# A list of background steps that is empty earns no steps

## The chip, the cores and the metric

One core of a Trainium2 chip runs the whole layer as one program. The metric is device time in microseconds, the median of several executions. The core has five engines that run side by side, each through its own instructions in order: TensorE (PE) for matmuls, VectorE (DVE), ScalarE (ACT), GpSimd (POOL) and SyncE (SP), which here only issues transfers. TensorE's clock is granted in two levels, 1.2 and 2.4 GHz; the profile gives the granted share of full speed.

## The reference

A decoder layer on 512 tokens of width 2048. With h the modulated RMS norm of x, one projection gives q, k, v (8 heads of 128), a forget logit, u (512 wide) and two gates:

```python
q, k, v, f_logit, u, gate_s, gate_a = jnp.split(h @ w_in, IN_SPLIT_POINTS, axis=-1)
y_ssm = half_glu(s5_mixer(u, ...))           # a scan over time, 1024 complex states
y_attn = fox_attention(q, k, v, f_logit, ...)  # head-wise RMS of q and k, causal softmax with a
                                               # bias from the cumulated log forget gate
merged = sigmoid(gate_s) * (y_ssm @ w_ssm_up) + sigmoid(gate_a) * (y_attn @ w_attn_up)
x = x + g1 * (merged @ w_out)
x = x + g2 * peer_ffn(h2, ...)               # product-key experts; most of the time, not touched here
```

## The kernel before, in words

A float32 matmul of the large projections is three matmuls (`mm3`, L88 to L90, and L201 to L203 for the token form): each operand is a rounded high part and the rest, and high x high, high x low and low x high are summed in PSUM.

The part around the change is written in an order by hand (`manual_schedule`): each engine gets its instructions in the order in which the program issues them. It begins after u is projected (about 160 us) and ends with the first pair of gates (about 773 us). Its trunk is the list of projections: the forget logits (`mproj(1)`), then for each of four pairs of heads q, k and v (`mproj_tok`, 256 columns, one result per 128 tokens), then two gates (`mproj(2)`). A projection runs in four units of weights; a unit's parts are quarters. A quarter of `mproj_tok` is 12 matmuls of 256 columns, one of `mproj(2)` 6 of 512. `unit` (L167) issues a part, behind the first part also the high part of the next unit's weights on ScalarE (L158) and their low part on VectorE (L164), and calls `tick` after each part. The stage has 8 + 12 x 16 + 32 = 232 ticks.

`tick` (L111) issues steps of background work. There are three lists (L1869 on), each `[generators, rate, credit]`; a step is what a generator does up to its next `yield`:
- `bpo`, rate 1: `forget` (L807, 11 steps) and `qk` (L838, 11 steps), the head-wise norm of q or k: squares on ScalarE (L846), the reciprocal root (L850 to L858) and the product (L861) on VectorE, eight transposes on TensorE (L867), copies on ScalarE.
- `bat`, rate RH, in the gates RL: two `head`s (L882, 14 steps each): scores on TensorE (L901), bias, mask and maximum on VectorE (L903 to L906), exp on ScalarE (L907), reciprocal (L912) and scaling (L913), transposes (L920), their copies (L922), products with v (L929), and a transfer to `yd` (L936).
- `bs5`, rate RT = 2.0 up to the end of the first q, then R5: the S5 scan (L687), 191 steps: tables, then 16 times (j) 10 steps of products, sums and scans on VectorE, four passes of `bu` (L724) and four of `y` (L732, L733) on TensorE.

q's list gets its generator when q's projection has been issued, k's likewise; the heads of a pair get theirs behind v (L1882). Just before, `flush` (L123) issues at once whatever is left in `bpo` and `bat`; at the end `bat` and `bs5` are flushed. Transposes, scores and the S5 transposes share two PSUM buffers (`tp`). Gelu of S5's result (L944) and the GLU belong to the next part, whose order a planner makes; the casts of the heads' outputs, read back from `yd` (L1899), stand at its start.

Of the kernel before, what the change touches and what calls it, by code (L numbers as in the profile page):

```python
# [38 lines left out]
TODO = ('tg', '', 'tgw', '', 'tg', '', 'tg', 'm')  # L39

RT = 2.0
R5 = 0.92
RH = 0.66
RL = 1.0
GB = (3592, 5640)
PE_ROWS = (2, 3, 5, 6, 7, 12)
NA = 3
# [16 lines left out]
class Builder:  # L64
# [46 lines left out]
    def tick(self):  # L111

        for b in self.bg:
            b[2] += b[1]
            while b[2] >= 1 and b[0]:
                b[2] -= 1
                try:
                    next(b[0][0])
                except StopIteration:
                    b[0].pop(0)  # L120
                    b[2] += 1
# [1002 lines left out]
    def routes(self, es, norm, rows, opened, early):  # L1124
# [45 lines left out]
        for h in range(NH):  # L1170
            pd = [self.t(pq, [P, TM], F32, "pd", bufs=3) for n in range(2)]
            pss = self.t(pq, [P, 256], F32, "ps", bufs=1)
            for j in range(4):
# [28 lines left out]
                for n in range(2):  # L1202
                    for k in range(4):
                        dense(n, k)
                    tick()
                for k in range(4):
                    first(k)
                tick()
            if h == 0:
                ep = opened()  # L1210
# [272 lines left out]
    def experts(self, route):  # L1483
# [5 lines left out]
        with ExitStack() as es:  # L1489
# [146 lines left out]
            def deferred(tick):  # L1636
                nonlocal n, nxt
                ga, nxt = scores(n, nxt, lambda c: tick())
                nc.sync.dma_start(self.gd[n], ga)
                n += 1  # L1640
# [190 lines left out]
    def build(self):  # L1831
# [26 lines left out]
        with tc.manual_schedule():  # L1858
# [15 lines left out]
            for hp in range(4):  # L1874
                qs, ks = [], []
                bpo[0].append(self.qk(self.raw(self.mproj_tok()), self.col2[:, 0:1], qs))
                bs5[1] = R5
                bpo[0].append(self.qk(self.raw(self.mproj_tok()), self.col2[:, 1:2], ks))
# [3 lines left out]
                bat[0].extend(self.head(hp * 2 + i, qs, ks, v) for i in range(2))  # L1882
            bat[1] = RL
            sg = self.gates(0, self.apool, "a")
# [93 lines left out]
```

## Time and profile before

| | us |
|---|---|
| median of 3 runs | 3901.11 (3896.51 to 3903.49) |
| the profiled execution, its own time | 3898.42 |
| its span, first to last instruction | 3896.6 |
| TensorE busy in the span | 3685.5 (95%) |
| VectorE busy | 3030.8 (78%) |
| ScalarE busy | 1305.8 (34%) |
| the stage of the change, 160.0 to 773.2 | 613.2 |
| TensorE busy in it, mean granted clock | 519.2, 0.88 |

Times in the trace are counted from the span's first instruction. A busy share of TensorE counts a matmul from its start to its modelled end, and at half clock a matmul takes twice as long, so the granted clock is read beside it. A wait is idle time of an engine directly before an instruction, put down to what released it last.

### The profile page before, as it was taken

The page shows a single profiled execution, that of the slowest core. Times are in us where ns is not written, and L with a number is a line of the kernel's source. Part 1 is how long each engine was busy: PE and PEld are TensorE (multiplying, and loading weights), DVE is VectorE, ACT ScalarE, POOL GpSimd, SP SyncE. Part 2 cuts the span into 40 slices and gives each one's busy share as a digit, 9 for nine tenths or more (in the row PEclk, how much of TensorE's full clock was granted, in tenths as well). Part 3 has the DMA queues.
Part 4 walks back from the last instruction along what each step waited for, and adds up shares of the span by engine and source line. Part 5 has one row for each costly group of instructions (what it writes and reads, how often), then busy time and mean ns, then how long its engine had stood idle before and what let it go on. Part 6 is the DMA issues. An engine that isn't in the chain of part 4 may idle for free.

```text
span 3896.6 us, 58629 instructions
## 1 busy us (share of the span) xinstructions
PE 3685.5 (95%) x22966; PEld 3375.0 (87%) x22966; DVE 3030.8 (78%) x4731; ACT 1305.8 (34%) x2265; POOL 725.8 (19%) x518
## 2 busy tenths in 40 slices
PE   6888888999999998899989999999999999999998
PEld 2677777777778778889989999999999999999997
DVE  6676665365657438986879999999999988999997
ACT  3323333422223224235644333333333333333332
POOL 0000000000000004423421222222222221222221
PEclk8998888899999999999999999999999999999999
DMA  8511112266777552227889999999999988999996
GB/s 300 178 55 49 49 49 71 76 211 213 219 219 230 157 139 89 69 94 261 299 299 309 327 363 372 367 362 366 372 368 371 369 308 298 369 372 356 371 367 216
DMA packets 467082, 967.39 MB, mean 248 GB/s; under 512 B 66379, under 2 KB 335861, under 8 KB 400117
## 3 DMA queue, kind: packets, MB, share of 16 engines
q1 hardware_dynamic: 411508, 560.97, 43.8%
q0 software_dynamic: 55296, 402.68, 26.6%
q8 instruction: 180, 2.95, 0.3%
q14 instruction: 98, 0.79, 0.1%
HBM read 926.51 MB, written 36.96 MB: 247 GB/s over the span
## 4 chain that ended last, share of the span: by engine, by line
PE 73%; DVE 12%; DMA 8%; ACT 3%; issue 2%; POOL 1%; SPq 0%; DVEq 0%; ACTq 0%; POOLq 0%
PE A L90 7%; PE A L88 7%; PE A L89 7%; PE V L90 7%; PE V L89 7%; PE V L88 7%; PE tp L1538 6%; DMA y<-in_w_ada_dram 5%; PE mm L201 2%; PE mm L203 2%; PE mm L202 2%; DVE y L301 2%; PE mm L88 2%; PE mm L90 2%; PE mm L89 2%
## 5 line engine op out<-in xcount | busy, mean ns | idle before, releaser
L88 PE MATMUL A<-hi,uhi 128*128 128x320 f32 x2048 | 658.1, 321 | 0.0
L88 PE MATMUL V<-ghi,vhi 128*128 128x320 f32 x2048 | 651.9, 318 | 3.3 <-ACT vhi L1518 2.7
L90 PE MATMUL V<-ghi,vlo 128*128 128x320 f32 x2048 | 633.9, 310 | 5.2 <-DVE vlo L1521 5.2
L89 PE MATMUL V<-glo,vhi 128*128 128x320 f32 x2048 | 634.1, 310 | 1.6 <-DVE glo L1599 1.5
L90 PE MATMUL A<-hi,ulo 128*128 128x320 f32 x2048 | 633.4, 309 | 0.0
L89 PE MATMUL A<-lo,uhi 128*128 128x320 f32 x2048 | 633.0, 309 | 0.0
L1542 ACT CAST uhi<-tp 128x512 fp32r<-128x512 f32 x512 | 301.0, 588 | 606.4 <-PE tp L1538 602.7
L1448 DVE SCALAR_TENSOR_TENSOR big<-g,av,big 128x2048 f32<-128x2048 f32 x190 | 445.6, 2345 | 11.7 <-DMA g<-in_peer_v_dram,ids 6.8
L1436 DVE SCALAR_TENSOR_TENSOR g<-g,big 128x2048 f32<-128x2048 f32 x192 | 438.3, 2284 | 16.6 <-DMA big<-hx 6.6
L88 PEld LDWEIGHTS V<-ghi,vhi 128*128 128x128 f32 x2048 | 386.2, 189 | 5.9 <-ACT vhi L1518 3.0
L90 PEld LDWEIGHTS V<-ghi,vlo 128*128 128x128 f32 x2048 | 385.5, 188 | 5.6 <-DVE vlo L1521 5.6
L89 PEld LDWEIGHTS V<-glo,vhi 128*128 128x128 f32 x2048 | 386.4, 189 | 2.7 <-DVE glo L1599 2.6
L89 PEld LDWEIGHTS A<-lo,uhi 128*128 128x128 f32 x2048 | 386.4, 189 | 0.0
L88 PEld LDWEIGHTS A<-hi,uhi 128*128 128x128 f32 x2048 | 386.1, 189 | 0.0
L90 PEld LDWEIGHTS A<-hi,ulo 128*128 128x128 f32 x2048 | 385.1, 188 | 0.0
L1549 DVE TENSOR_TENSOR ulo<-tp,uhi 128x512 fp32r<-128x512 f32 x428 | 291.3, 681 | 58.6 <-ACT uhi L1542 49.8
L94 ACT CAST whi<-wf 128x1024 fp32r<-128x1024 f32 x146 | 153.6, 1052 | 540.3 <-PE mx L89 217.4
L1521 DVE TENSOR_TENSOR vlo<-vf,vhi 128x1024 fp32r<-128x1024 f32 x248 | 302.5, 1220 | 28.2 <-ACT vhi L1518 28.0
L1518 ACT CAST vhi<-vf 128x1024 fp32r<-128x1024 f32 x248 | 259.6, 1047 | 165.4 <-PE V L89 132.5
L1538 PE MATMUL tp<-ident,uf 128*128 128x128 f32 x2048 | 307.7, 273 | 5.0 <-DMA uf<-in_peer_u_dram 4.7
L301 DVE SCALAR_TENSOR_TENSOR y<-y,cond,y 128x512 f32<-128x512 f32 x240 | 192.9, 804 | 148.4 <-DMA y<-in_w_ada_dram 145.3
L1538 PEld LDWEIGHTS tp<-ident,uf 128*128 128x128 f32 x2048 | 255.6, 141 | 15.5 <-issue 5.1
(470 smaller groups left out, 7359.0 us busy)
## 6 DMA issues: line engine op xcount, KB each, us to landing
uf<-in_peer_u_dram SPq DMA_DIRECT2D x128, 1024.0 KB
vf<-in_peer_v_dram SPq DMA_DIRECT2D x248, 512.0 KB
y<-in_w_ada_dram SPq DMA_DIRECT2D x256, 256.0 KB
wf<-in_w_in_dram SPq DMA_DIRECT2D x116, 512.0 KB
wd<-ev SPq DMA_DIRECT2D x40, 512.0 KB
wt<-wd SPq DMA_DIRECT2D x128, 160.0 KB
adaw<-in_w_ada_dram SPq DMA_DIRECT2D x32, 512.0 KB
wf<-in_w_ada_dram SPq DMA_DIRECT2D x32, 512.0 KB
```

The costliest lines, as they stand in the source:

```text
L88: mm(ps, lhi, rhi, start=start, stop=False)
L89: mm(ps, lhi, rlo, start=False, stop=False)
L90: mm(ps, llo, rhi, start=False, stop=stop)
L94: nc.scalar.copy(hi, src)
L301: nc.vector.scalar_tensor_tensor(acc, w, col, acc, op0=ALU.mult, op1=ALU.add)
L1436: V.scalar_tensor_tensor(g, g, 1.0, hr, op0=ALU.mult, op1=ALU.mult, accum_out=av[:, s:s + 1])
L1448: V.scalar_tensor_tensor(acc, g, av[:, s:s + 1], acc, op0=ALU.mult, op1=ALU.add)
L1518: nc.scalar.copy(vhi, vf)
L1521: V.tensor_sub(vlo, vf, vhi.bitcast(F32))
L1538: mm(tp[:, k], ufs[i][:, (4 * c + k) * P:(4 * c + k + 1) * P], self.ident, is_transpose=True, start=k == 0, stop=False, skip_group_check=True)
L1542: nc.scalar.copy(hi, tp)
L1549: late.append(on_pe if i < ND0 - 3 else lambda: V.tensor_sub(lo, tp, hi.bitcast(F32)))
```

## The change

Credit is added only while a list has a generator; while it is empty its credit is 0. Two rates change with it.

```diff
-R5 = 0.92
+R5 = 0.8
 RH = 0.66
-RL = 1.0
+RL = 1.1
...
     def tick(self):
 
         for b in self.bg:
-            b[2] += b[1]
+            b[2] = b[2] + b[1] if b[0] else 0.0
             while b[2] >= 1 and b[0]:
                 b[2] -= 1
                 try:
```

## Rows read from the trace of the kernel before

**Rows 1.** The page: TensorE's granted clock in 40 slices of the span, in tenths.

```profile
PEclk8998888899999999999999999999999999999999
```

**Rows 2.** Busy time by stretch: its length, then each engine (instructions), PEclk, DMA share, GB/s.

```profile
160.00:773.20 613.20, 519.22 (x3083) 435.78 (x3082) 362.30 (x838) 213.94 (x492) 0.00 (x0) 0.88 0.19 59
178.00:229.00 51.00, 34.41 (x195) 27.79 (x194) 44.12 (x97) 14.28 (x40) 0.00 (x0) 0.85 0.14 41
299.20:332.50 33.30, 23.92 (x83) 15.48 (x81) 17.18 (x42) 17.00 (x43) 0.00 (x0) 0.70 0.02 9
...
729.60:773.20 43.60, 43.60 (x189) 35.10 (x188) 15.90 (x19) 16.94 (x24) 0.00 (x0) 1.00 0.38 115
773.20:1240.00 466.80, 459.08 (x2004) 369.65 (x2003) 291.64 (x364) 112.90 (x131) 26.09 (x14) 1.00 0.69 214
```

**Rows 3.** Waits of TensorE, 160 to 773 us: total us, times, longest.

```profile
PE tp L867 <- DVE t L861: 44.9, 8, 7.4
PE tp L901 <- DVE S L903: 13.9, 8, 1.7
PE tp L920 <- ACT PT L922: 11.3, 9, 1.4
...
PE tp L824 <- DVE fz L818: 4.1, 1, 4.1
```

**Rows 4.** Timeline of TensorE in the second pair's heads: start, us, instruction, idle before.

```profile
439.12 2.08 PE L901 MATMUL tp<-a,a 128*128 128x512 f32 x2 [1.73 <-DVE S L903]
```

**Rows 5.** Busy time as in rows 2, a stretch of token projection alone.

```profile
676.00:696.00 20.00, 20.00 (x168) 19.91 (x167) 3.80 (x4) 4.02 (x5) 0.00 (x0) 1.00 0.27 82
```

**Rows 6.** The chain of waits, 240 to 260 us: start, us, what.

```profile
244.13 1.72 PE bu L724 x4
...
257.35 0.86 PE y L732 x2
```

**Rows 7.** Instructions of VectorE by line, 160 to 773 us: busy us, mean ns, idle before.

```profile
L164 DVE TENSOR_TENSOR wlo<-wf,whi 128x1024 fp32r<-128x1024 f32 (+1 forms) x59 | 70.5, 1195 | 99.2 <-ACT whi L158 99.2
L773 DVE TENSOR_TENSOR_SCAN w<-s5mag,car,w 128x128 f32<-128x128 f32 x48 | 22.9, 478 | 0.0
L903 DVE SCALAR_TENSOR_TENSOR S<-tp,cq,nc 128x128 f32<-128x128 f32 (+3 forms) x32 | 17.3, 541 | 49.8 <-ACT nc L891 48.2 <-PE tp L901 1.6
L906 DVE TENSOR_REDUCE sm<-S 128x1 f32<-128x128 f32 (+3 forms) x32 | 15.6, 486 | 1.1
...
L757 DVE TENSOR_TENSOR w<-w,tmv 128x512 f32<-128x512 f32 x16 | 11.0, 690 | 0.4
...
L754 DVE TENSOR_TENSOR tmv<-bu,stab 128x512 f32<-128x512 f32 x16 | 10.9, 684 | 3.3 <-PE bu L724 3.3
...
L780 DVE SCALAR_TENSOR_TENSOR car<-w,s5p6c,car 128x1 f32<-128x1 f32 x48 | 10.5, 220 | 0.0
...
L861 DVE TENSOR_TENSOR t<-t,ms 128x512 f32<-128x512 f32 x16 | 10.3, 688 | 0.3
...
L905 DVE TENSOR_TENSOR S<-S,mask 128x128 f32<-128x128 f32 x32 | 9.3, 292 | 1.1
...
L912 DVE RECIPROCAL sm<-sm 128x1 f32<-128x1 f32 x32 | 5.2, 164 | 24.1 <-ACT S L907 24.1
```

**Rows 8.** Waits of ScalarE, 160 to 773 us, as in rows 3.

```profile
ACT a L944 <- DVE a L737: 12.0, 3, 4.6
```

**Rows 9.** Timeline of SyncE's issues, 729 to 735 us: start, us, issue.

```profile
730.18 0.34 SPq L936 DMA_DIRECT2D yd<-yo  x1
...
733.81 0.92 SPq L1899 DMA_DIRECT2D sg<-yd  x2
```

**Rows 10.** Instructions of ScalarE by line, 160 to 773 us, as in rows 7.

```profile
L907 ACT ACT_TABLE_LOAD x4 | 5.1, 1283 | 0.1
...
L94 ACT CAST y<-sg 128x512 fp32r<-128x512 f32 x8 | 4.4, 620 | 2.3 <-DMA yd<-yo 2.3
```

## The prediction

> **What bounds the kernel now.** I began with the page's row of the granted TensorE clock [rows 1]: it is 9 nearly everywhere after slice 10, and lower and uneven in slices 3 to 8, about 200 to 780 us. So I cut that part into stretches by what the projections do [rows 2]. In the stretch of a head pair (299.2 to 332.5) TensorE is busy 23.92 of 33.30 us at a mean clock of 0.70, VectorE 17.18 and ScalarE 17.00: no engine is full, they wait for each other in turn. There are four such stretches, 33.3, 33.4, 32.9 and 32.6 us (the first is shown). Right behind it the gate projection alone keeps TensorE busy 43.60 of 43.60 us at clock 1.00, and after 773 us TensorE is busy 459 of 467 us. The waits of TensorE from 160 to 773 us [rows 3] name the places: 44.9 us in 8 waits of the q and k transposes for VectorE (at most 7.4 us each), 13.9 and 11.3 us inside the heads, 4.1 us in the forget gate. The timeline of the second burst [rows 4] shows the pattern: a score stands 1.73 us until VectorE has read the score before it, and so on through the chain of a head. So TensorE, which works in order, has other work in hand (the next quarter of a projection), and stands because the whole of a head or of q is queued ahead of that work.
>
> Why it is queued in one piece is read from the code. The credit of a list (b[2]) grows at every tick, also while the list is empty. Ticks: 8 in the forget projection, 16 in each of 12 token projections, 32 in the gates, 232 in all. By the first heads 56 ticks have paid 56 x 0.66 = 37 credits; two heads have 28 steps; so all 28 come in one tick. For q, 16 ticks pay 16 credits for 11 steps: also one tick. The trace agrees: 8 waits for 8 q and k lists, four bursts for four pairs.
>
> **The change part by part.** An empty list now earns nothing. Counting steps by hand: the forget gate's 11 steps take 11 ticks, q and k take 11 of the 16 ticks they have, a pair's 28 steps at 0.66 are done in tick 43 of 48, and the last pair, at 1.1, in tick 26 of the gates' 32. S5 has 191 steps; 48 come in the first 24 ticks at 2.0, as before, the other 143 at 0.8 need 179 ticks instead of 155 at 0.92, and end in tick 203, four ticks into the gates. So no flush has anything left. No work is added or removed; its order on the three engines changes.
>
> Prices on TensorE at full clock: a 256-column matmul of a projection 20.00 / 168 = 0.119 us [rows 5], a 512-column one 43.60 / 189 = 0.231 us [rows 2], one j of S5 1.72 + 2 x 0.86 = 3.44 us [rows 6]. A head at full clock is not in the trace, it always runs in a burst. Bounds: its 2560 + 1024 + 3840 columns at S5's 1.72 / 2048 us per column give 6.2 us; a burst's busy time without any recovery gives 23.92 / 2 = 12.0 us. I take 7.4 per head, 14.8 per pair, near the lower end, because the passes of 128 columns may not reach S5's rate but the clock will be high when projections stand between them. VectorE: a j of S5 is 8 products of 0.684, 4 sums of 0.69, 8 scans (about 0.45) and the carries, 14.1 us; a head 4 x (0.541 + 0.486 + 0.292 + 0.164) + 0.2 = 6.1 us; a q or k about 2.3 us; a weight's low part 1.22 us [rows 7].
>
> Now by stretches, saved time positive.
> A, 178 to 229 us, first ticks with S5 at 2.0: VectorE is busy 44.1 of 51 us [rows 2], so it is nearly the bound. The forget wait (4.1) and the first q wait go, but not below VectorE's work. I take 5 us; bounds 2 and 7.
> B, 229 to 299.2 us, 32 ticks: 384 x 0.119 = 45.7, S5 2.6 j = 8.8, transposes 2, together 56.5; plus 3 for the VectorE backlog from A. Against 70.2: 10.7 saved.
> C, 299.2 to 697 us, three times 48 ticks: 576 x 0.119 = 68.5, S5 3.84 j = 13.2, a pair of heads 14.8, q and k and the S5 transposes 2.5, together 99 us. VectorE in the same 48 ticks: 54 for S5, 12.2 heads, 4.6 q and k, 14.6 low parts, together 85 us. So TensorE would stay the bound at 86% VectorE. What is late next: both PSUM buffers tp are shared by heads, q, k and S5's transposes, and where S5 and a score meet in a tick the second waits for VectorE; and VectorE's reciprocal waits for ScalarE's exp (24.1 us before 32 reciprocals now [rows 7]) with S5 work queued behind it. I charge 6 us per 48 ticks (below 0: not; above: the second rival). 3 x 105 = 315 against 397.8: 83 saved.
> D, 697 to 773.2 us: 192 x 0.231 = 44.4, heads 14.8, the last S5 steps 1, together 60, plus 5 for the end: now the last head's output is written in the last ticks of the gates, the reload from DRAM is issued 3.6 us after it, and eight casts of 0.62 us follow it [rows 9, 10] before the GLU's own; that tail lay under 43.6 us of projection, now under some 8. 65 against 76.2: 11 saved.
> Last, gelu of u sits in ScalarE's queue and already held it 12.0 us in three waits for S5 [rows 8]; nothing behind it was late, since the heads came in one piece. Now exp stands behind it: minus 3 us (bounds 0 and minus 10). SyncE only gets its yd writes later; weight loads are 3 deep and DMA is busy 0.02 to 0.38 in these stretches [rows 2], so it hides them. What follows 773 us (99% TensorE) moves up as it is.
> Sum: 5 + 10.7 + 83 + 11 - 3 = about 106 us. The profiled execution takes 3898.4 us, 2.7 under the median of the runs. 3898.4 - 106 = 3792, by the median 3795 us.
>
> The clock is the term on which C rests. In the burst the clock is 0.70 although TensorE is 72% busy; in the projections that follow each other without a wait it is 1.00 [rows 2, 5]. The Trainium skill (TensorE: Matmul & The Clock Gate, "A second HAM failure mode: psum-queue depth-cycling") warns that frequent short idles between groups of matmuls make the clock oscillate, which speaks against spreading steps that each may wait a little. The burst bears this out; whether a step between quarters does so too, no row shows, and the third rival prices it.
>
> **Rivals.** First, the forecast: steps spread, waits nearly gone.
> Second, VectorE becomes the bound in C. If each of a pair's 8 reciprocals still holds VectorE as a score's wait held TensorE in the burst (13.9 / 8 = 1.7 us [rows 3]; the exp and sqrt tables now alternate, 1.28 us a load [rows 10]), that is 14 us per 48 ticks: VectorE fills 99 of 105, and the period grows to about 119. Then 3 x 14 = 42 less is saved, 64 in all, 3837 us. For it: 86% load with serial waits. Against: S5's steps stand between most head steps.
> Third, slower: every step's short wait holds the clock at 1.2 GHz through C. At half clock 48 ticks are at most 2 x 99 = 198 us, against 132.6 now: 3 x 65 = 196 lost, 27 still saved in A, B and D: up to 4070 us. It decides from the point where 0.36 of C's TensorE work is at half clock, 106 / (3 x 99). For it: the burst's clock. Against: a quarter of 12 matmuls (1.4 us) lies behind each step, busy by itself.
> Fourth, the change doesn't do what it says, since a flush still finds the lists full: about 3895 us. By the count above it shouldn't.
> Fifth, the gain is given back behind 773 us, where a planner orders the gates, ada and merge around the weights: those stretches are 99% busy, so at most part; some 50 us left, 3850.
>
> **Numbers.** Forecast 0.72, second 0.14, third 0.05, fourth 0.03, fifth 0.06. What a measurement can tell from no change is about 0.2%, 8 us. Faster 0.92, same 0.03, slower 0.05. The time is the forecast's, 3795. The range goes down to 3762, where C has no extra waits (18), heads cost 6.2 (10) and the tail nothing (5), and up to 3850, which takes in the second rival and most of the fifth.
>
> **What would show it.** TensorE's waits for L861 fall from 44.9 to a few us, those inside the heads (13.9 and 11.3 the largest) to under 10 in all; the stretch from 160 us to the first GLU matmul falls from 613 to about 507 us at a clock of 0.97 or more; VectorE's busy share there rises from 0.59 to about 0.71; the exp table loads rise from 4 [rows 10] to about 7. Head transposes appear singly between projection matmuls. Wrong if the clock there stays under 0.9 (third rival), if VectorE is busy over 90% in 48-tick stretches with TensorE waiting for it (second), or if the stretch shrinks and the total does not (fifth).

## The result, and the profile after

The changed kernel takes 3757.39 us (median of 4 runs, 3745.4 to 3761.35) against 3898.81 us before in the same runs: ratio 0.9637, 95% interval 0.9605 to 0.9668, 141 us less. The forecast was 106 us less, 3795 us, and the range ended at 3762: the direction and the mechanism came out, the size was a quarter too small. All times are of fast executions: the second of the two of the kernel called e7 below, 4441.11 us at a granted clock of 0.75, was slow and is left out.

The page's clock row and the busy time by stretch of the changed kernel (columns as in [rows 2]; the stretches: the whole stage; from the first q projection to the second quarter of the first k; on to the second q; the three times 48 ticks of C; the gates; what follows):

```profile
PEclk8999999999999999999999999999999999999999
```

```profile
160.00:631.90 471.90, 456.07 (x3079) 394.70 (x3077) 356.13 (x835) 219.67 (x501) 0.00 (x0) 0.99 0.25 77
172.40:214.90 42.50, 35.19 (x230) 29.20 (x229) 40.04 (x84) 13.50 (x25) 0.00 (x0) 0.92 0.21 62
214.90:270.70 55.80, 55.35 (x412) 50.31 (x411) 50.17 (x119) 22.04 (x60) 0.00 (x0) 1.00 0.26 76
270.70:563.80 293.10, 292.34 (x2116) 260.09 (x2115) 228.69 (x554) 140.98 (x340) 0.00 (x0) 1.00 0.23 71
563.80:631.90 68.10, 61.46 (x279) 45.95 (x277) 28.51 (x53) 39.75 (x73) 0.00 (x0) 1.00 0.33 103
632.00:1100.00 468.00, 462.25 (x2002) 371.82 (x2003) 294.17 (x368) 112.60 (x132) 26.10 (x14) 0.99 0.68 213
```

Against [rows 2] the stage went from 613.2 to 471.9 us, 141.3 less. TensorE's idle time in it fell from 94.0 (613.2 - 519.2) to 15.8 us, 78 less; its busy time from 519.2 to 456.1, 63 less, with the same matmuls, at a clock of 0.99 in place of 0.88. So the gain is waits and half clock, a little over half of it waits. In C TensorE stands still for 0.8 of 293 us. Behind the stage nothing changed: the next 468 us are as full as they were. The profiled execution was the fastest of its runs: its span is 153 us under the one before, and 12 of them lie behind the stage, as executions of one kernel differ.

The waits of TensorE in the stage (total us, times, longest), as in [rows 3]:

```profile
PE tp L713 <- ACT bt L708: 6.7, 2, 6.1
PE mm L88 <- issue: 4.0, 1, 4.0
PE tp L901 <- DVE S L903: 0.9, 1, 0.9
```

These are the two largest and the one that is left of the scores' 13.9 us; each other row is under 1 us. The row of L867, 44.9 us before, is gone, and so are the forget gate's 4.1. The largest waits are now at S5's first transposes and before the GLU. The timeline of TensorE shows a score of the first head between two quarters; the projection's last and first matmul stand directly beside it:

```profile
284.08 0.28 PE L203 MATMUL mm<-whi,h 128*128 128x256 f32 x1
284.19 0.59 PE L901 MATMUL tp<-a,a 128*128 128x256 f32 x2
284.44 0.47 PE L201 MATMUL mm<-whi,h 128*128 128x256 f32 x1
```

### The profile page after: what moved, and what is told of

Same layout as the page of the kernel before. It is cut to its first block, busy times and chain, and to the rows that moved or that the text cites. A ratio compares the mean times of both kernels' runs of the same rounds, so it can differ in the third digit from the quotient of the medians.

```text
span 3743.6 us, 58621 instructions
## 1 busy us (share of the span) xinstructions
PE 3619.8 (97%) x22966; PEld 3332.4 (89%) x22966; DVE 3020.2 (81%) x4731; ACT 1311.5 (35%) x2274; POOL 726.2 (19%) x518
## 4 chain that ended last, share of the span: by engine, by line
PE 77%; DVE 11%; DMA 8%; issue 2%; ACT 2%; POOL 1%; SPq 0%; DVEq 0%; ACTq 0%; POOLq 0%
PE A L88 8%; PE A L90 8%; PE A L89 8%; PE V L90 8%; PE V L89 8%; PE V L88 8%; PE tp L1538 6%; DMA y<-in_w_ada_dram 5%; PE mm L89 2%; PE mm L88 2%; PE mm L90 2%; PE mm L201 2%; PE mm L202 2%; PE mm L203 2%; DVE y L301 2%
## 5 line engine op out<-in xcount | busy, mean ns | idle before, releaser
L88 PE MATMUL mm<-h,whi 128*128 128x512 f32 x656 | 264.6, 403 | 0.7 <-ACT a L517 0.7
```

The lines of the kernel that those rows point to most:

```text
L88: mm(ps, lhi, rhi, start=start, stop=False)
```

## The experiments

Beside each whole time I read one length from the trace: from the first matmul of the first q projection to the first matmul of the GLU. It is 599.8 us before (173.5 to 773.3) and 459.4 after (172.4 to 631.9), and was 459.4 again in a second profile of the changed kernel (e9), while whole executions of one kernel differ by some 10 us. It is called the stage length below.

**The credit line alone (e1).**

```diff
-R5 = 0.8
+R5 = 0.92
-RL = 1.1
+RL = 1.0
```

> The changed kernel with the two rates of before (R5 0.92, RL 1.0): the credit line alone. Theory A (the gain is the bursts' waits and the half clock they bring; VectorE may lag behind TensorE by several ticks without TensorE noticing, so its load does not matter below 100%): in 48 ticks VectorE has 62 us of S5 + 12.2 + 4.6 + 14.6 = 93.6, TensorE 68.5 + 15.2 + 13 = 97; no new waits, and only the heads end two ticks later in the gates. 138 us under the kernel before, ratio 0.9645. Theory B (lowering R5 is what makes room on VectorE; at 0.92 it is 96% loaded and TensorE waits 5 us or more in each 48 ticks): 120 to 125 us under, ratio 0.969.

Measured: 3751.98 us, ratio 0.9656 (0.9624 to 0.9689), some 134 us under the kernel before by the ratio; stage length 461.0. In the same three times 48 ticks:

```profile
268.20:562.80 294.60, 292.44 (x2115) 259.79 (x2114) 226.21 (x546) 141.93 (x337) 0.00 (x0) 1.00 0.25 76
```

The wall time is 294.6 against 293.1 us, no wait of weight. The interval of the whole times ends just short of theory B's 0.969, and the rows are far from it: theory B wanted 15 us of waits here, TensorE idles 2.2. The credit line is the change; the rates add nothing to speak of.

**Heads alone (e2), forget, q and k alone (e3), rates alone (e4).** Each keeps the credit of the other lists:

```diff
-            b[2] = b[2] + b[1] if b[0] else 0.0
+            b[2] = b[2] + b[1] if b[0] or b is self.bg[0] else 0.0    # e2
+            b[2] = b[2] + b[1] if b[0] or b is self.bg[1] else 0.0    # e3
+            b[2] += b[1]                                              # e4
```

> The changed kernel, but the list of forget, q and k keeps its credit while empty: only the heads are spread. Theory A: the parts add up. The changed kernel's marks by projection give 88 us saved in the three projections that held a burst of heads (28.9 + 32.2 + 26.7) and 10 in the gates, less some 12 us of head work that now lies in the k and v projections: about 76 us under the kernel before, ratio 0.9805. Theory C (the parts are not independent: one kind of burst left is enough to keep the clock down between them): under 50 us, ratio over 0.987.

> The changed kernel, but the list of heads keeps its credit while empty: only forget, q and k are spread. Theory A: the rest of the gain, 141 - 76 = 65 us under the kernel before (8 waits of 44.9 us and 4.1, and the half clock behind each), ratio 0.983. Theory C: under 45 us.

> The kernel before with the two new rates (R5 0.8, RL 1.1), all credit kept. Theory A: bursts as before, S5 ends in tick 203 in place of 179; within 8 us of the kernel before, ratio 0.998 to 1.002. Theory B: some of the gain, 15 us or more under.

| | ratio (95%) | stage length | shorter by |
|---|---|---|---|
| heads alone | 0.9856 (0.9827 to 0.9884) | 539.8 | 60.0 |
| forget, q, k alone | 0.9815 (0.9781 to 0.9848) | 529.6 | 70.2 |
| rates alone | 0.9996 (0.9985 to 1.0008) | 594.9 | 4.9 |

The two parts make 130 of 140.4 us, and each has the two new rates in it, which alone make 4.9; so they nearly add, and neither needs the other. By the stage lengths theory C falls; the whole times of the heads alone, 45 to 67 us under the kernel before, would leave it room. The rates alone come out as theory A had it. The sizes of the two parts were the other way round than expected (76 and 65): with only the heads spread, each q or k still comes in one piece, and TensorE waits 12.9 us longer for these pieces. The largest wait of e2, 44.9 us in [rows 3]:

```profile
PE tp L867 <- DVE t L861: 57.8, 8, 8.9
```

What stands ahead of the piece is ScalarE's head work. At the three longest waits, 8.9 us each, an exp runs on ScalarE in front of the piece's copies and squares, and VectorE, at its next instruction, stands some 4 us for the squares (the first of the three):

```profile
365.99 0.72 ACT L907 ACTIVATE S<-S,sm 128x512 f32<-128x512 f32 x1 [1.19 <-DVE sm L906]
371.07 0.17 DVE L850 TENSOR_SCALAR ms<-ms 128x8 f32<-128x8 f32 x1 [3.80 <-ACT jk L846]
```

After exp the table of the square root has to be loaded again: seven loads of 1.28 us in front of the eight roots (L851), five in the kernel before.

**Two head steps in a tick (e5).** `RH = 2.0`.

> The changed kernel with RH = 2.0: two head steps in each tick, a pair done in 14 of 48 ticks. It measures how much distance a step needs. Theory A (a step's chain of score, bias and maximum, exp, reciprocal, scaling takes some 3 us, as in the burst; TensorE has no wait as long as two or three ticks of 1.5 to 2 us lie between a score and its transposes): with one tick between them TensorE waits about 1 us in most of the 7 ticks of a head, 10 us per pair and some half clock, for the three pairs at RH 20 to 40 us longer than the changed kernel's stage of 472 us. Theory D (one quarter behind a step is enough, however many steps it holds): within 5 us of 472.

Measured: 3775.21 us, ratio 0.968 (0.9634 to 0.9727), 18 to 23 us over the changed kernel by its two medians (3757.39 and 3752.06); stage length 481.0, 21.6 longer. That is theory A's number, at its low end. C in that kernel, and TensorE's largest waits in C:

```profile
269.70:584.30 314.60, 301.11 (x2116) 264.49 (x2115) 228.95 (x553) 136.85 (x335) 0.00 (x0) 0.98 0.23 66
```

```profile
PE tp L901 <- DVE S L903: 4.6, 3, 2.0
PE tp L920 <- ACT PT L922: 3.5, 6, 0.8
PE tp L713 <- DVE S L903: 2.2, 1, 2.2
```

VectorE does the same 229 us as in the changed kernel. TensorE idles 13.5 us in place of 0.8, and another 9 us is busy time at a clock of 0.98 in place of 1.00. But the waits are not those that theory A reasoned with. Each of the 14 (three smaller rows are 1.5, 1.2 and 0.4 us) is of an instruction that writes `tp`, a score or a transpose of a head or of S5, and it ends when VectorE or ScalarE has read an earlier result out of `tp`. None is a transpose that waits for its scaled scores (L913); in the bursts of the kernel before there were 8 of those, 8.1 us. So it is not the distance between a score and its transposes that got too short: with two head steps in a tick, and S5's transposes beside them, the two `tp` buffers are wanted again before they have been read.

**S5 faster, VectorE loaded (e6).** `R5 = 1.3`.

> The changed kernel with R5 = 1.3: S5 ends in tick 134. From tick 24 to 134 VectorE has 202 us of S5 + 34 low parts + 22 heads + 16 q and k = 274 us, TensorE 157 + 49 + 16 + 10 = 232 us. Theory A (VectorE's load costs nothing below 100%, the excess above it comes through less a lag of about 14 us, one j of S5): the stage is 25 to 30 us longer than the changed kernel's 472. Theory B (VectorE's waits for exp and TensorE's waits for VectorE rise steadily with load): about 5 us at 0.92 and 45 or more here.

Measured: 3757.59 us, ratio 0.9635 (0.959 to 0.968); stage length 469.0, 9.6 longer, under both theories. The ticks 24 to 136 and the largest waits of TensorE there:

```profile
214.10:464.90 250.80, 242.54 (x1640) 205.00 (x1639) 241.42 (x602) 109.90 (x264) 0.00 (x0) 0.99 0.23 67
```

```profile
PE y L733 <- DVE s L799: 4.4, 4, 2.3
PE tp L867 <- DVE t L861: 3.1, 2, 2.3
```

VectorE is busy 96% of the time, and TensorE waits 8 us for it. The expected 274 us of VectorE work were a sum of durations. Those recorded in this stretch add up to 276 us too, but they overlap, and the busy time is 241.4. So the load had been overestimated, and at 96% it costs TensorE some 3% of the stretch.

**The GLU before the reloads (e7).**

```diff
+        ys = self.half_glu()
         yh = []
         for h in range(NH):
...
-        ys = self.half_glu()
```

> The changed kernel with the GLU issued before the eight reloads of the heads' outputs. In the changed kernel TensorE waits about 5 us before the GLU's first matmul for casts that stand behind the reloaded heads, and then runs some 4 us at half clock. If that tail is what the gates lost, the stage from the first gate matmul to the first GLU matmul falls from 68.0 to 62 or 63 us and the wait is gone; if the wait is set by S5's or gelu's end, nothing changes.

Measured by the profile alone (its execution 3757.78 us, from which 4 us can't be told): the gates take 63.8 us in place of 68.0, a little more than the 62 or 63 expected, and the 4.0 us wait before the GLU is gone. So the changed kernel's tail is the eight casts of the heads' outputs ahead of the GLU's own.

**Filler in the waits (e8).** In the kernel before, `qk`:

```diff
             ps = self.t(self.ptp, [P, S], F32, "tp")
+            for i in range(18 if h == 0 else 0):
+                hi = self.h[i % KT][0]
+                nc.tensor.matmul(ps, hi[:, 0:P], hi, start=True, stop=True)
             for t in range(TT):
```

> The kernel before with 18 extra matmuls of 512 columns (4.2 us at full clock) ahead of the eight transposes of each q and k, into the PSUM buffer that the transposes then overwrite: work added, no result changed. Eight waits of 4.2 to 7.4 us there are filled for the most part. Theory A (a good part of the loss is not the wait but the half clock behind it: TensorE's busy time in the stage fell from 519.2 to 456.1 us with the same work): the clock stays up behind these eight places, 2.5 to 3 us each, and the kernel is 15 to 25 us faster though it does more, ratio 0.994 to 0.996. Theory E (only waiting counts): no faster, ratio 1.000, or slower where 4.2 us does not fit.

Measured: 3878.76 us, ratio 0.9965 (0.9955 to 0.9975), 14 us faster with 144 matmuls more. Stage length 587.4, 12.4 shorter; the granted clock in it 0.92 in place of 0.88:

```profile
160.00:758.20 598.20, 535.55 (x3220) 447.65 (x3219) 361.85 (x838) 212.01 (x491) 0.00 (x0) 0.92 0.21 60
```

In the 7 us behind the first of the eight places the clock was 0.72 in the kernel before (230.4 to 237.4 us, 46 matmuls) and is 1.00 here (227.1 to 234.1, 53 matmuls). The gain is a little below what was expected, and clearly not theory E's 1.000: the half clock behind a wait costs time of its own, about 12 us / 8 = 1.5 us for each of the eight places.

**A better version (e9 to e11).** e10 is the changed kernel with the GLU first and S5's fills ahead of its tables (the first diff; the GLU's edit is e7's); e11 adds an evener S5 (the second):

```diff
-        yield from self.s5_tables()
...
             V.memset(x, 0.0)
         yield
+        yield from self.s5_tables()
```

```diff
-RT = 2.0
-R5 = 0.8
+RT = 1.5
+R5 = 0.85
```

> The changed kernel once more, for the comparison with the next one on the same chip: ratio to the kernel before 0.9637 as in the result.

> The changed kernel with the GLU issued before the reloads (as in e7, 4 us off the gates) and S5's four fills with zeros issued before its tables instead of behind them, so that the copies of its first transposed matrices do not wait 6.5 us for VectorE, and TensorE not 6.7 us for them. If the first q projection then loses that wait and some half clock: its 41.0 us fall to 33 to 36, and the stage is 9 to 12 us under the changed kernel's 459.4 us (first q matmul to first GLU matmul); the time 0.25% under it. If VectorE, busy 36 of 38.6 us there, is the bound, only the GLU's 4 us are left.

> The kernel of e10 with S5 spread more evenly: RT 1.5 in the first 24 ticks, R5 0.85 behind them (it ends in tick 206). In e10 VectorE is busy 40.2 of 41.0 us in the first q projection and TensorE 35.4. Theory A (at S5's rate 2.0 VectorE's load is over 100% there and comes through to TensorE; at 1.5 it is below, and at 0.85 behind it still only some 80%): the first q projection falls from 40.6 to 32 to 35 us, the projections behind it grow by under 2 us in all, and the stage falls from 454.2 to 447 to 450 us; the time 0.3% under the changed kernel, ratio 0.9605. Rival: the 40.6 us are set by the chain through S5's first j and not by VectorE's load; then q stays above 38 us.

| | median us | ratio (95%) | stage length | first q projection |
|---|---|---|---|---|
| e9, the changed kernel | 3752.06 | 0.9637 (0.9624 to 0.965) | 459.4 | 41.0 |
| e10 | 3746.75 | 0.9638 (0.9624 to 0.9651) | 454.2 | 40.6 |
| e11 | 3747.49 | 0.9629 (0.9611 to 0.9647) | 448.9 | 30.7 |

In e10 the 6.7 us wait for S5's first copies is gone, and the first q projection is no shorter: VectorE is the bound there, busy 39.88 of 40.60 us (e10; then e11, the first q projection of each):

```profile
170.70:211.30 40.60, 34.97 (x217) 29.12 (x216) 39.88 (x86) 12.24 (x23) 0.00 (x0) 0.92 0.23 65
169.90:200.60 30.70, 28.90 (x209) 26.52 (x208) 28.39 (x55) 13.46 (x25) 0.00 (x0) 0.94 0.30 86
```

With S5 at 1.5 steps a tick (e11) it takes 30.7 us, VectorE is busy 92% of it, and the stage is 10.5 us under the changed kernel's. The lower rate thins VectorE's load and also draws out the chain of S5's first j, so e11 does not tell these two apart; the row of e10 speaks for the load. The rest of the stage got 4.5 us longer than in e10, where under 2 were expected, and the ratio stayed above the 0.9605 that was expected. The whole times can't tell the three apart: their intervals overlap, and what follows the stage took 3112 to 3132 us in single profiles of these kernels. So e11 is better in the stage, and not shown to be faster.

## Why the prediction fell short

**Right.** What bounds the stage, the count of steps (no flush found anything: the S5 scan ends in the gates, the last head in their 26th tick), that TensorE stays the engine that sets the time, and that the clock stays up. VectorE is busy 0.75 of the stage, where 0.71 was forecast. The third rival (half clock through C) did not come: its condition, a short wait at each step, is absent, and the granted clock in C is 1.00. The Trainium skill (TensorE: Matmul & The Clock Gate, "A second HAM failure mode: psum-queue depth-cycling") warns of frequent short idles between groups of matmuls. The trace of e5 agrees, if weakly: with 14 waits of 0.1 to 2.2 us in C its clock there is 0.98, and with a single one of 0.4 us, in the changed kernel, 1.00.

**By stretches**, saved us. A is taken here from the start of the stage to TensorE's second quarter of the first k (230.4 us before, 214.9 after), B from there to the second q (67.4 us long before, 55.8 after), then C (397.7 and 293.1) and the gates (77.7 and 68.0):

| | predicted | measured |
|---|---|---|
| A | 5 (2 to 7) | 15.5 |
| B | 10.7 | 11.6 |
| C | 83 | 104.6 |
| D, with gelu | 8 | 9.7 |
| sum | 106 | 141.4 |

**The step that failed** is the charge for the lists meeting, "I charge 6 us per 48 ticks (below 0: not; above: the second rival)", and, from the same thought, VectorE's work as a floor in A, "but not below VectorE's work. I take 5 us; bounds 2 and 7". In C the charge was 18 us; measured, TensorE idles 0.8. In A 15.5 us were saved (1.1 of them ahead of the first q projection, where the kernels are alike), more than twice the upper bound. Together that is some 28 of the 35 us that the forecast missed.

The charge in C named two things. One is steps that meet at the two `tp` buffers: in C of the changed kernel TensorE waits for them once, 0.4 us. The other is VectorE's reciprocal behind ScalarE's exp, 24.1 us in the stage before, 7.8 after, and of those in C:

```profile
DVE sm L912 <- ACT S L907: 0.7, 1, 0.7
```

The first is real where the buffers are wanted more often: it is 13.4 of the 13.5 us that e5 idles in C with two head steps in a tick. So the charge had to be worked out from how many steps want a buffer in a tick, and at 0.66 head steps it comes to nearly nothing.

Under the charge lay a load that was read too high. VectorE's "together 85 us" per 48 ticks, "86%", is a sum of recorded durations, and these overlap. In the changed kernel two products of S5 start 0.60 us apart while each is recorded with 0.68 (start, us):

```profile
290.10 0.68 DVE L754 TENSOR_TENSOR tmv<-bu,stab 128x512 f32<-128x512 f32 x1
290.70 0.68 DVE L755 TENSOR_TENSOR w<-bu,ctab 128x512 f32<-128x512 f32 x1
```

VectorE's recorded durations in C add up to 257.5 us, 86 per 48 ticks as forecast, but its busy time is 228.7 / 3 = 76 us, 78% of 97.7. With the right load the charge would have been nearly as wrong: even at 96% (e6) TensorE waits only 8 us in 251.

In A the row before, beside that after in the result, is:

```profile
173.50:230.40 56.90, 40.31 (x238) 33.29 (x236) 47.51 (x102) 18.24 (x44) 0.00 (x0) 0.85 0.16 47
```

TensorE's idle time fell by 9.3 us (the two waits that the forecast names, 4.1 and 6.0, went) and its busy time by 5.1, at a clock of 0.92 in place of 0.85. VectorE's 44.1 of 51 us were no floor: it is busy 40.04 us in A after, in place of 47.51, and does part of its work in B instead (50.17 in place of 46.60), where TensorE is busy 55.35 of 55.8 us and does not wait for it. VectorE does bound the first q projection (e10, e11), at 41 us; the forecast had put that bound too high. The 3 us for "the VectorE backlog from A" in B did not come either: B took 55.8 us against 56.5 without them.

**Smaller terms.** TensorE's work in C is 292.3 / 3 = 97.4 us per 48 ticks against 99; with the other terms as they were that leaves some 6.6 us per head in place of 7.4 (an estimate: no run shows a head's work by itself). The tail was given 5 us, the gates idle 6.6 (68.1 - 61.5). Gelu's minus 3 us did not come: ScalarE waits 5.5 us there in place of 12.0, and nothing behind it was late. The exp tables are loaded 10 times, not 7, each 1.28 us; TensorE's waits show nothing of it.

The second rival's mechanism was tested by its extreme (e6) and needs a load near 100%. Its price did not follow from its own condition: 99 us of VectorE's work fit in a period of 105, so they give no period of 119. The range failed with the same step: its lower end took away C's 18 us and the heads' and tail's margins, and left the floor in A standing.

Two readings were off, and nothing hangs on them. The row of the clock [rows 1] is below 9 in slices 4 to 8 (292 to 779 us) and in slice 1, not in 3 to 8; and TensorE's share right behind 773 us is 98% (459.08 of 466.80 us), not 99%.

## What to carry to other kernels

Where work is paced by credit, look at what an empty list earns: a bank of steps comes out as one burst, in which an in-order engine waits through a chain of three engines while its own work stands behind. When such a chain is spread, count how many steps want the same buffers within one tick, and look whether they have been read by then. Take another engine's load as a union of its busy time and not as a sum of durations; here 96% of it cost TensorE 8 us in 251. Count a wait on TensorE at more than its length if the granted clock falls behind it.

## What had not been expected of the hardware

Adding 144 matmuls in front of eight waits made the kernel 14 us faster (e8, ratio 0.9965, 0.9955 to 0.9975). Of the 141 us that the change brought, 63 are TensorE's busy time with the same matmuls. VectorE starts its next product of 128 x 512 before the recorded end of the last, 0.60 us apart for 0.68 us each.
